# A bitonic sort of 2^18 keys on one core: mirrored merges, signs folded into the layout changes, and layout changes in quarters

## The chip, the cores and the metric

The kernel runs on one core of one Trainium2 chip. The metric is the time of one execution in microseconds (us), measured on the device. Every number below is a median over several executions, unless it is read from a profile; a profile shows one execution, and its span (first to last instruction) is about 2 us shorter than the measured time of the same execution.

Names: PE is TensorE for matmuls and PEld its weight loads, DVE is VectorE, ACT is ScalarE, POOL is GpSimd, SP is SyncE.

## The reference, cut to what matters

```python
N, E, D = 4096, 262144, 256
self_out = nodes @ w_self
msg = nodes[edges_src] @ w_msg
agg = np.zeros((N, D), np.float32)
np.add.at(agg, edges_dst, msg)          # a scatter-add over 262144 random edges
return self_out + agg
```

The kernel has no fast scatter-add. It packs every edge into one float key (destination and source bits), sorts the 262144 keys, and then walks over chunks of 128 sorted edges. For each chunk it builds two one-hot matrices on DVE and multiplies them on PE (the "one-hot stage"). The change concerns the sort, and what stands directly before and after it.

## The kernel before: the parts that matter

The keys lie in a tile of 128 partitions x 2048. In layout A a row (partition) holds 2048 neighbouring keys, so compare-exchange passes over index bits 0 to 10 are DVE work along a row. In layout B each 128x128 block is transposed, so bits 7 and higher lie along the row. Stage s of the bitonic sort merges over bits s-1 down to 0; from stage 11 on, the top bits need layout B and the low seven need layout A.

```python
def evac(out_ap, in_ap, g):                    # out of PSUM: ACT and DVE in turn
    if g % 2 == 0: nc.scalar.copy(out=out_ap, in_=in_ap)
    else:          nc.vector.tensor_copy(out=out_ap, in_=in_ap)

def switch_A_to_B():                           # switch_B_to_A is alike
    src = buf("A")
    dst3 = buf("B").rearrange("q (p g) -> q p g", g=G16)
    for g in range(G16):                       # 16 blocks of 128x128
        tp = psum.tile([P, P], FP32, name="tp_sw", tag="tp", bufs=4)
        nc.tensor.transpose(tp[:], src[:, g * P:(g + 1) * P], ident[:])
        evac(dst3[:, :, g], tp[:], g)

def flip(lay, blo, bhi):                       # negate half the keys, so that every
    ...                                        # comparison can run upwards
    nc.vector.tensor_scalar(out=reg, in0=reg, scalar1=-1.0, scalar2=None, op0=ALU.mult)

def cpass(lay, fb):                            # one pass: a min and a max, 128x1024 each
    ...
    nc.vector.tensor_tensor(out=lo_d, in0=lo_s, in1=hi_s, op=ALU.min)
    nc.vector.tensor_tensor(out=hi_d, in0=lo_s, in1=hi_s, op=ALU.max)

for s in range(1, NSTAGE + 1):                 # NSTAGE 18, JBITS 11
    if s <= JBITS - 1:
        flip("A", ...)
        for b in range(s - 1, -1, -1): cpass("A", b)
    else:
        switch_A_to_B(); flip("B", ...)
        for b in range(s - 1, 6, -1): cpass("B", b - 7)
        switch_B_to_A()
        for b in range(6, -1, -1): cpass("A", b)
switch_A_to_B()
```

After the sort, the first key of every 128-key chunk gives segment numbers. These go through DRAM to every partition; ACT counts signs; the counts become row indices; GpSimd gathers two sets of rows ("heads", `xh`); then the one-hot stage starts with the heads. A validity check of the kernel (`bad`, `bcol`, then a small DRAM round trip `fd` to `brow`, then `bsum`) stands in the same region.

Of the kernel before, what the change touches and what calls it, by code (L numbers as in the profile page):

```python
# [9 lines left out]
P = 128  # L10
FP32 = mybir.dt.float32
BF16 = mybir.dt.bfloat16
I32 = mybir.dt.int32
I64 = mybir.dt.int64

ALU = mybir.AluOpType
AX = mybir.AxisListType
ACTF = mybir.ActivationFunctionType
# [18 lines left out]
def _view3(ap: bass.AP, inner: int):  # L37
    return ap.rearrange("p (a b) -> p a b", b=inner)
# [3 lines left out]
def kernel(  # L42
# [9 lines left out]
    nc = tc.nc  # L52
# [4 lines left out]
    NCOL = E // P  # L57
# [3 lines left out]
    NSTAGE = 18  # L61
    JBITS = 11
    G16 = NCOL // P

    const = ctx.enter_context(tc.tile_pool(name="const", bufs=1))
    feat = ctx.enter_context(tc.tile_pool(name="feat", bufs=1))
    meta = ctx.enter_context(tc.tile_pool(name="meta", bufs=1))
# [10 lines left out]
    ident = const.tile([P, P], FP32, name="ident")  # L78
# [4 lines left out]
    Y = feat.tile([P, T, D], BF16, name="Y")  # L83


    sortp = tc.alloc_tile_pool(name="sortp", bufs=1)
    XA = [sortp.tile([P, NCOL], FP32, name=f"XA{i}") for i in range(2)]
    XB = [sortp.tile([P, NCOL], FP32, name=f"XB{i}") for i in range(2)]

    HC = NCOL // 2  # L90
    for h in range(2):
        d64 = XB[0][:].bitcast(I64)
        s64 = XB[1][:].bitcast(I64)
        nc.sync.dma_start(
            d64, edges_dst.rearrange("(p j) -> p j", p=P)[:, h * HC:(h + 1) * HC]
        )
        nc.scalar.dma_start(
            s64, edges_src.rearrange("(p j) -> p j", p=P)[:, h * HC:(h + 1) * HC]
        )
        dlo = d64.bitcast(I32)[:, 0::2]  # L100
        slo = s64.bitcast(I32)[:, 0::2]
        hi = XA[1][:].bitcast(I32)
        dhi = hi[:, 0:HC]
        shi = hi[:, HC:2 * HC]
        key = XA[0][:, h * HC:(h + 1) * HC]
        nc.vector.tensor_single_scalar(out=dhi, in_=dlo, scalar=9, op=ALU.logical_shift_right)
        nc.vector.tensor_single_scalar(out=shi, in_=slo, scalar=7, op=ALU.logical_shift_right)
        nc.vector.scalar_tensor_tensor(
            out=key, in0=dlo, scalar=128.0, in1=slo, op0=ALU.mult, op1=ALU.add
        )  # L110
        nc.vector.scalar_tensor_tensor(
            out=key, in0=dhi, scalar=float((1 << 21) - (1 << 16)), in1=key,
            op0=ALU.mult, op1=ALU.add,
        )
        nc.vector.scalar_tensor_tensor(
            out=key, in0=shi, scalar=float((1 << 16) - P), in1=key,
            op0=ALU.mult, op1=ALU.add,
        )


    ones_sent = const.tile([1, 1], FP32, name="ones_sent")
# [19 lines left out]
        out=hbase[:], in0=hbase[:], scalar1=float(SEGW), scalar2=None, op0=ALU.mult  # L141
# [6 lines left out]
        out=thr[:], in0=thr[:], scalar1=float(SEGW), scalar2=-0.5, op0=ALU.mult, op1=ALU.add  # L148
# [11 lines left out]
        pattern=[[0, NPER], [1, RING], [0, 8]], base=0, channel_multiplier=0,  # L160
# [19 lines left out]
    for t in range(T):  # L180
        y_ps = psum_y.tile([P, D], FP32, name="y_ps", tag="y_ps", bufs=2)
        for k in range(2):
            nc.tensor.matmul(  # L183
                out=y_ps[:], lhsT=XT[:, k, t * P:(t + 1) * P], rhs=wcat[:, 2 + k, :],
                start=(k == 0), stop=(k == 1),
            )
        nc.scalar.copy(out=Y[:, t, :], in_=y_ps[:])  # L187

    psum_sort = tc.alloc_tile_pool(name="psum_sort", bufs=1, space=bass.MemoryType.PSUM)
    srt, lane = _run_sort(nc, psum_sort, XA, XB, ident, NCOL, NSTAGE, JBITS, G16)  # L190


    k16 = meta.tile([P, G16], FP32, name="k16")
    k16i = meta.tile([P, G16], I32, name="k16i")
    kn = meta.tile([P, G16], FP32, name="kn")
    kni = meta.tile([P, G16], I32, name="kni")
# [13 lines left out]
    cnt = meta.tile([P, 2], FP32, name="cnt")  # L210
    cidx = meta.tile([P, 2], I32, name="cidx")

    tss = nc.vector.tensor_single_scalar
    tt = nc.vector.tensor_tensor
    nc.scalar.dma_start(xs_dram.rearrange("(p g) l -> p (g l)", g=G16), srt[:])
    nc.vector.tensor_copy(out=k16i[:], in_=srt[:, 0::P])
    tss(out=gi[:], in_=k16i[:], scalar=7, op=ALU.logical_shift_right)
    tss(out=dl[:], in_=gi[:], scalar=SEGW - 1, op=ALU.bitwise_and)
    nc.vector.tensor_scalar(
# [30 lines left out]
    rel_b = meta.tile([P, NCOL], BF16, name="rel_b")  # L250
    for q in range(NCOL // SBL):
        s = slice(q * SBL, (q + 1) * SBL)
        nc.vector.tensor_copy(out=ki[:, s], in_=lane[:, s])
        tss(out=kl[:, s], in_=ki[:, s], scalar=P - 1, op=ALU.bitwise_and)
        nc.scalar.copy(out=slo_b[:, s], in_=kl[:, s])
        tss(out=ki[:, s], in_=ki[:, s], scalar=7, op=ALU.logical_shift_right)
# [17 lines left out]
    for h in range(2):  # L274
        xh = meta.tile([P, P], FP32, name=f"xh{h}")
        nc.gpsimd.indirect_dma_start(
            out=xh[:], out_offset=None, in_=xs_dram[:, :],
            in_offset=bass.IndirectOffsetOnAxis(ap=cidx[:, h:h + 1], axis=0),
        )
        xt_ps = psum_sort.tile([P, P], FP32, name="xt_ps", tag="tp", bufs=4)  # L280
        nc.tensor.transpose(xt_ps[:], xh[:], ident[:])
        nc.vector.tensor_copy(out=hs_i[:, h * P:(h + 1) * P], in_=xt_ps[:])
    tss(out=hd_i[:], in_=hs_i[:], scalar=7, op=ALU.logical_shift_right)
    tss(out=hs_i[:], in_=hs_i[:], scalar=P - 1, op=ALU.bitwise_and)
    nc.vector.tensor_copy(out=hsl[:], in_=hs_i[:])
# [1 line left out]
    psum_sort.release()  # L287
    psum_y.release()
    stgn.release()
    sortp.release()  # L290

    for q in range(NCOL // SBL):
# [127 lines left out]
    brow = meta.tile([1, P], FP32, name="brow")  # L420
    bsum = meta.tile([1, 1], FP32, name="bsum")
    flag = meta.tile([1, 1], I32, name="flag")
    nc.vector.tensor_copy(out=k16[:], in_=k16i[:])
    nc.sync.dma_start(kd[0, 0:NCOL].rearrange("(p g) -> p g", g=G16), k16[:])
    nc.sync.dma_start(kn[:], kd[0, 1:NCOL + 1].rearrange("(p g) -> p g", g=G16))
    nc.vector.tensor_copy(out=kni[:], in_=kn[:])
# [88 lines left out]
            )  # L515


def _run_sort(nc, psum, XA, XB, ident, NCOL, NSTAGE, JBITS, G16):

    cur = {"A": 0, "B": 0}  # L520

    def buf(lay):
        return XA[cur[lay]][:, 0:NCOL] if lay == "A" else XB[cur[lay]][:, 0:NCOL]

    def other(lay):
        return XA[1 - cur[lay]][:, 0:NCOL] if lay == "A" else XB[1 - cur[lay]][:, 0:NCOL]

    def flip_live(lay):
        cur[lay] = 1 - cur[lay]

    def evac(out_ap, in_ap, g):
        if g % 2 == 0:
            nc.scalar.copy(out=out_ap, in_=in_ap)  # L533
        else:
            nc.vector.tensor_copy(out=out_ap, in_=in_ap)

    def switch_A_to_B():
        src = buf("A")
        dst3 = buf("B").rearrange("q (p g) -> q p g", g=G16)
        for g in range(G16):  # L540
            tp = psum.tile([P, P], FP32, name="tp_sw", tag="tp", bufs=4)
            nc.tensor.transpose(tp[:], src[:, g * P:(g + 1) * P], ident[:])  # L542
            evac(dst3[:, :, g], tp[:], g)

    def switch_B_to_A():
        src3 = buf("B").rearrange("q (p g) -> q p g", g=G16)
        dst = buf("A")
        for g in range(G16):
            tp = psum.tile([P, P], FP32, name="tp_sw2", tag="tp", bufs=4)
            nc.tensor.transpose(tp[:], src3[:, :, g], ident[:])  # L550
            evac(dst[:, g * P:(g + 1) * P], tp[:], g)

    def flip(lay, blo, bhi):
        x = buf(lay)
        if lay == "A":
            assert blo <= JBITS - 1 and (bhi is None or bhi <= JBITS - 1)
            base_lo = blo
        else:
            assert blo >= 7
            base_lo = blo - 7  # L560
            if bhi is not None:
                assert bhi == blo + 1
        if bhi is None:
            per = 1 << (base_lo + 1)
            reg = _view3(x, per)[:, :, (1 << base_lo):per]
        else:
            per = 1 << (base_lo + 2)
            reg = _view3(x, per)[:, :, (1 << base_lo):(3 << base_lo)]
        nc.vector.tensor_scalar(out=reg, in0=reg, scalar1=-1.0, scalar2=None, op0=ALU.mult)

    def cpass(lay, fb):
        src = buf(lay)
        dst = other(lay)
        per = 1 << (fb + 1)
        s3 = _view3(src, per)
        d3 = _view3(dst, per)
        lo_s = s3[:, :, 0:(1 << fb)]
        hi_s = s3[:, :, (1 << fb):per]
        lo_d = d3[:, :, 0:(1 << fb)]
        hi_d = d3[:, :, (1 << fb):per]  # L580
        nc.vector.tensor_tensor(out=lo_d, in0=lo_s, in1=hi_s, op=ALU.min)  # L581
        nc.vector.tensor_tensor(out=hi_d, in0=lo_s, in1=hi_s, op=ALU.max)  # L582
        flip_live(lay)

    for s in range(1, NSTAGE + 1):
        if s <= JBITS - 1:
            if s == 1:
                flip("A", 1, None)
            else:
                flip("A", s - 1, s)  # L590
            for b in range(s - 1, -1, -1):
                cpass("A", b)
        else:
            switch_A_to_B()
            if s == NSTAGE:
                flip("B", NSTAGE - 1, None)
            else:
                flip("B", s - 1, s)
            for b in range(s - 1, 6, -1):
                cpass("B", b - 7)  # L600
            switch_B_to_A()
            for b in range(6, -1, -1):
                cpass("A", b)

    switch_A_to_B()
    return XA[cur["A"]], XB[cur["B"]]


# [28 lines left out]
```

## Time and profile before

Time: 842.63 us (median of 3 runs, 841.58 to 842.98). The profiled execution has a span of 841.4 us.

These are two lines of the page's part 1 and part 2 for the kernel before. The first gives busy time, share of the span and instruction count per engine. The second is the TensorE clock that was granted, in tenths of full speed (9 is 90% or more), in 40 slices of 21 us each.

```profile
PE 337.7 (40%) x3730; PEld 268.0 (32%) x3730; DVE 772.9 (92%) x851; ACT 221.6 (26%) x449; POOL 15.1 (2%) x24
...
PEclk9999999999555555555555555589999999999999
```

DVE is busy 92% of the time, so DVE is the engine to relieve. The run of 5s says that PE works at about half clock from 210 us to the end of the sort. The clock is recorded only from its first rise on, here at 203 us, and what lies before that is shown as 9. The three switches before 203 us show the same spacing of their transposes, about 0.215 us, as those under the 5s, so they too ran at half clock.

A switch in detail: rows of the timeline of the kernel before (start in us, duration in us, engine, line, operation, output <- input). The last pass in layout B, two of the sixteen transposes, the last copy out of PSUM, and the first instruction of the next pass.

```profile
175.62 1.23 DVE L581 TENSOR_TENSOR XB_86<-XB_87 128x1024 f32<-128x1024 f32 x1
176.76 1.22 DVE L582 TENSOR_TENSOR XB_86<-XB_87 128x1024 f32<-128x1024 f32 x1
...
178.52 0.42 PE L550 MATMUL tp_sw_527<-ident,XB_86 128*128 128x128 f32 x1
...
178.74 0.42 PE L550 MATMUL tp_sw_530<-ident,XB_86 128*128 128x128 f32 x1
...
181.76 0.29 DVE L535 COPY XA_85<-tp_sw_563 128x128 f32<-128x128 f32 x1 [0.32 <-PE tp_sw_563 L550]
182.15 1.23 DVE L581 TENSOR_TENSOR XA_84<-XA_85 128x1024 f32<-128x1024 f32 x1
```

A pass repeats every 2.395 us (409.5 us for all 171). The pass at 175.62 would therefore be followed by another at 178.01; the next one comes at 182.15. So this B-to-A switch costs 4.14 us. An A-to-B switch costs 4.54, and a sign flip 0.73 beyond that. The transposes come every 0.21 to 0.22 us.

| part of the kernel before | us | how it is read |
|---|---|---|
| start, to the first flip | 24.0 | timeline |
| 171 passes | 409.5 | 171 x 2.395 |
| 18 flips | 13.1 | 18 x 0.73 |
| 16 layout switches | 69.4 | 8 x 4.14 + 8 x 4.54 |
| end of the last pass to the one-hots of the heads | 28.6 | 516.0 to 544.61 |
| one-hot stage | 296.8 | 544.61 to 841.4 |

Two more rows of the timeline of the kernel before, at the start: the shift L106 of the first key half waits 8.25 us for its load, and the first flip begins at 24.00.

```profile
8.25 1.31 DVE L106 TENSOR_SCALAR XA_85<-XB_86 128x1024 int32<-128x1024 int32 x1 [8.25 <-DMA XB_86<-in_edges_dst_dram]
...
24.00 0.70 DVE L569 TENSOR_SCALAR XA_84<-XA_84 128x1024 f32<-128x1024 f32 x1
```

And three at the end: the gather of the heads, the transpose that had to wait for its data, and the one-hot that ends the latency chain.

```profile
534.15 1.09 POOL L276 DMA_INDIRECT xh_1583<-xs_dram,cidx  x1 [520.10 <-DVE cidx L267]
...
541.62 0.45 PE L281 MATMUL xt_ps<-ident,xh_1583 128*128 128x128 f32 x1 [20.16 <-DMA xh_1583<-xs_dram,cidx]
...
544.61 1.20 DVE L310 TENSOR_TENSOR e_oh<-hsl,jrow 128x2048 bf16<-128x2048 bf16 x1
```

### The profile page before, as it was taken

The page shows a single profiled execution, that of the slowest core. Times are in us where ns is not written, and L with a number is a line of the kernel's source. Part 1 is how long each engine was busy: PE and PEld are TensorE (multiplying, and loading weights), DVE is VectorE, ACT ScalarE, POOL GpSimd, SP SyncE. Part 2 cuts the span into 40 slices and gives each one's busy share as a digit, 9 for nine tenths or more (in the row PEclk, how much of TensorE's full clock was granted, in tenths as well). Part 3 has the DMA queues.
Part 4 walks back from the last instruction along what each step waited for, and adds up shares of the span by engine and source line. Part 5 has one row for each costly group of instructions (what it writes and reads, how often), then busy time and mean ns, then how long its engine had stood idle before and what let it go on. Part 6 is the DMA issues. An engine that isn't in the chain of part 4 may idle for free. (4 is left out here: it accounts for less than half of the span.)

```text
span 841.4 us, 9662 instructions
## 1 busy us (share of the span) xinstructions
PE 337.7 (40%) x3730; PEld 268.0 (32%) x3730; DVE 772.9 (92%) x851; ACT 221.6 (26%) x449; POOL 15.1 (2%) x24
## 2 busy tenths in 40 slices
PE   0033320111111111111101112088888888888786
PEld 0000000111111111111101111076776777777675
DVE  3999999999999999999999998599999999999995
ACT  0011110111111111111101111245555555555454
POOL 6000000000000000000000000000000000000000
PEclk9999999999555555555555555589999999999999
DMA  8811100000000000000000002000000000000000
GB/s 238 177 27 25 27 19 0 0 1 1 0 0 0 0 0 0 1 0 0 0 0 0 0 0 102 7 2 26 3 27 2 26 2 27 26 2 26 2 26 28
DMA packets 25209, 17.89 MB, mean 21 GB/s; under 512 B 11557, under 2 KB 24358, under 8 KB 24390
## 3 DMA queue, kind: packets, MB, share of 16 engines
q1 hardware_dynamic: 19862, 11.59, 4.6%
q0 software_dynamic: 4720, 2.49, 2.2%
q10 hardware_dynamic: 578, 3.16, 0.9%
q8 instruction: 31, 0.51, 0.2%
q14 instruction: 18, 0.15, 0.1%
HBM read 10.12 MB, written 7.37 MB: 21 GB/s over the span
## 5 line engine op out<-in xcount | busy, mean ns | idle before, releaser
L342 ACT CAST at<-ring 128x512 bf16<-128x512 f32 x256 | 150.0, 587 | 144.9 <-PE ring L326 144.8
L326 PE MATMUL ring<-d_oh,e_oh 128*128 128x96 bf16 x2304 | 147.5, 208 | 44.6 <-DVE d_oh L310 38.4
L368 PE MATMUL out_ps<-Y,at 128*128 128x256 bf16 x1024 | 154.8, 274 | 0.0
L310 DVE TENSOR_TENSOR e_oh<-slo_b,jrow 128x2048 bf16<-128x2048 bf16 x128 | 154.3, 1206 | 0.0
L326 PEld LDWEIGHTS <-e_oh 128*128 128x128 bf16 x2304 | 132.2, 99 | 66.6 <-issue 48.1
L310 DVE TENSOR_TENSOR d_oh<-rel_b,jrow 128x1536 bf16<-128x1536 bf16 x128 | 120.3, 940 | 0.0
L368 PEld LDWEIGHTS <-at 128*128 128x128 bf16 x1024 | 86.5, 97 | 7.4 <-ACT at L342 0.6
L581 DVE TENSOR_TENSOR XA_85<-XA_84 128x1024 f32<-128x1024 f32 x56 | 68.6, 1225 | 2.2
L581 DVE TENSOR_TENSOR XA_84<-XA_85 128x1024 f32<-128x1024 f32 x55 | 67.4, 1225 | 2.2
L582 DVE TENSOR_TENSOR XA_85<-XA_84 128x1024 f32<-128x1024 f32 x56 | 68.3, 1219 | 0.0
L582 DVE TENSOR_TENSOR XA_84<-XA_85 128x1024 f32<-128x1024 f32 x55 | 67.0, 1219 | 0.0
L542 PE MATMUL tp_sw<-ident,XA_85 128*128 128x128 f32 x80 | 20.5, 436 | 111.3 <-DVE XA_85 L582 110.6
L183 PE MATMUL y_ps<-wcat,XT 128*128 128x256 bf16 x64 | 25.2, 394 | 96.3 <-DMA XT<-nodes_bf_dram 96.3
L542 PEld LDWEIGHTS tp_sw<-ident,XA_85 128*128 128x128 f32 x80 | 14.3, 193 | 117.4 <-DVE XA_85 L582 70.1
L533 ACT COPY XB_86<-tp_sw 128x128 f32<-128x128 f32 x40 | 15.1, 379 | 117.8 <-PE tp_sw L542 115.3
L542 PE MATMUL tp_sw<-ident,XA_84 128*128 128x128 f32 x64 | 16.0, 434 | 68.9 <-DVE XA_84 L582 68.9
L183 PEld LDWEIGHTS <-XT 128*128 128x128 bf16 x64 | 6.7, 104 | 114.6 <-DMA XT<-nodes_bf_dram 114.6
L581 DVE TENSOR_TENSOR XB_86<-XB_87 128x1024 f32<-128x1024 f32 x30 | 36.8, 1225 | 1.0
L581 DVE TENSOR_TENSOR XB_87<-XB_86 128x1024 f32<-128x1024 f32 x30 | 36.8, 1225 | 1.0
L187 ACT CAST Y<-y_ps 128x256 bf16<-128x256 f32 x32 | 11.9, 372 | 96.8 <-PE y_ps L183 96.8
L582 DVE TENSOR_TENSOR XB_87<-XB_86 128x1024 f32<-128x1024 f32 x30 | 36.6, 1219 | 0.0
L582 DVE TENSOR_TENSOR XB_86<-XB_87 128x1024 f32<-128x1024 f32 x30 | 36.6, 1219 | 0.0
(478 smaller groups left out, 287.3 us busy)
## 6 DMA issues: line engine op xcount, KB each, us to landing
out_dram<-o_sb SPq DMA_DIRECT2D x16, 256.0 KB, 2.3
XB_87<-in_edges_src_dram ACTq DMA_DIRECT2D x2, 1024.0 KB, 7.6
XB_86<-in_edges_dst_dram SPq DMA_DIRECT2D x2, 1024.0 KB, 7.5
nodes_bf<-in_nodes_dram POOLq DMA_DIRECT2D x1, 2048.0 KB, 18.1
nodes_bf_dram<-nodes_bf SPq DMA_DIRECT2D x1, 2048.0 KB, 8.7
XT<-nodes_bf_dram SPq DMA_TRANSPOSE x64, 2.4
xs_dram<-XA_85 ACTq DMA_DIRECT2D x1, 1024.0 KB
gball<-gd SPq DMA_DIRECT2D x1, 1024.0 KB, 4.7
```

The lines of the kernel that those rows point to most:

```text
L183: nc.tensor.matmul(out=y_ps[:], lhsT=XT[:, k, t * P:(t + 1) * P], rhs=wcat[:, 2 + k, :], start=(k == 0), stop=(k == 1),)
L187: nc.scalar.copy(out=Y[:, t, :], in_=y_ps[:])
L310: tt(out=o[:], in0=val.rearrange("p (g i) -> p g i", i=2).unsqueeze(2).to_broadcast(shp), in1=jrow[:, 0:wid, :].unsqueeze(1).to_broadcast( ...
L326: mm = nc.tensor.matmul(out=ap, lhsT=e[:, ci // 2, :, ci % 2], rhs=d[:, ci // 2, :, ci % 2], start=start, stop=True, skip_group_check=True ...
L342: ins = nc.scalar.copy(out=at[:], in_=ring[:, b:b + SEGW]).ins
L368: nc.tensor.matmul(out=out_ps[:, t, :], lhsT=at[:, t * P:(t + 1) * P], rhs=Y[:, b, :], start=False, stop=(b == T - 1), skip_group_check=True,)
L533: nc.scalar.copy(out=out_ap, in_=in_ap)
L542: nc.tensor.transpose(tp[:], src[:, g * P:(g + 1) * P], ident[:])
L581: nc.vector.tensor_tensor(out=lo_d, in0=lo_s, in1=hi_s, op=ALU.min)
L582: nc.vector.tensor_tensor(out=hi_d, in0=lo_s, in1=hi_s, op=ALU.max)
```

## The change

The intent has five parts:

- **No flips.** In layout A the first pass of a merge reads its second half backwards (a "mirrored" merge), so nothing has to be negated. For merges that begin in layout B the sign changes between stages are folded into the matrix that transposes: seven signed identities `sids`. The starting signs go into the key building (`ksg`).
- **Stage 11 inside a row.** The row merges now reach stage 11, which takes away one pair of switches.
- **No passes inside a chunk.** The order within 128 edges does not matter to the one-hot stage. The last merge stops after bit 7, and only the minimum of each chunk is taken after one last switch back. That takes away seven passes.
- **Switches in quarters.** The pass before a switch and the one after it are each split in four. Four plain f32 matmuls fill one PSUM bank (128x512), ACT copies it out in one instruction, and DVE starts on that quarter while PE works on the next.
- **Separate load buffers** for the two halves of the edges.

The core of the diff, cut, with some statements joined into fewer lines (`...` marks cuts):

```diff
+    for k in range(7):
+        nc.gpsimd.tensor_scalar(out=sids[k][:], in0=ident[:], scalar1=sgn[:, k:k + 1],
+                                scalar2=None, op0=ALU.mult)
...
+        nc.scalar.activation(out=key, in_=slo, func=ACTF.Copy, scale=ksg[:, 0:1])
+        tss(out=dhi, in_=dlo, scalar=9, op=ALU.logical_shift_right)
+        tss(out=shi, in_=slo, scalar=7, op=ALU.logical_shift_right)
+        for v, i in ((dlo, 1), (dhi, 2), (shi, 3)):
+            nc.vector.scalar_tensor_tensor(out=key, in0=v, scalar=ksg[:, i:i + 1], in1=key, ...)
...
+    for q in range(4):
+        _switch(nc, psum_sort, lane, srt, ident, q)
+        nc.vector.tensor_reduce(out=k16[:, 4 * q:4 * q + 4],
+            in_=_view3(srt[:, q * 512:(q + 1) * 512], P), axis=AX.X, op=ALU.min)
...
+def _switch(nc, psum, src, dst, rhs, q):
+    tp = psum.tile([P, 512], FP32, name="tp_sw", tag="tp", bufs=4)
+    for k in range(4):
+        c = slice((4 * q + k) * P, (4 * q + k + 1) * P)
+        nc.tensor.matmul(out=tp[:, k * P:(k + 1) * P], lhsT=src[:, c], rhs=rhs[:], start=True, stop=True)
+    nc.scalar.copy(out=dst[:, q * 512:(q + 1) * 512], in_=tp[:])
...
+    def cpass(src, dst, b, mirror=False, split=1):
+        ...
+            hi = s4[:, :, 1, ::-1] if mirror else s4[:, :, 1, :]
...
+    for s in range(1, JBITS + 1):                       # row merges, stages 1 to 11
+        for b in range(s - 1, -1, -1):
+            last = s == JBITS and b == 0
+            cpass(XA[a], XA[1 - a], b, mirror=(b == s - 1), split=4 if last else 1)
+    for s in range(JBITS + 1, NSTAGE + 1):              # stages 12 to 18
+        for q in range(4): _switch(nc, psum, XA[a], XB[b_], sids[s - JBITS - 1], q)
+        ...  cpass in B, first and last with split=4
+        if s == NSTAGE: return XB[b_]
+        for q in range(4): _switch(nc, psum, XB[b_], XA[a], ident, q)
+        for b in range(6, -1, -1): cpass(XA[a], XA[1 - a], b, split=4 if b in (0, 6) else 1)
```

After the change there are 164 passes and 13 switches in the sort, plus the last switch back for the minima.

## The prediction

It was written before the changed kernel had been run.

> **What bounds the kernel now.** By busy time per engine, VectorE (DVE) is busy 92% of 841 us. The timeline shows three stages. (1) To 24 us: load and key building, with DVE idle 8.3 and 4.9 us for loads. (2) 24 to 516: the sort, DVE in strict sequence. 171 passes of min+max (128x1024 f32, 1.22 us busy each, one pass every 2.395 us) = 409.5 us; 18 sign flips of 0.69 (pitch 0.73) = 13 us; 16 layout switches. From the last max to the next pass a B-to-A switch costs 4.1 us, an A-to-B switch 4.5 without its flip: 69 us. Sum 24+409.5+13+69 = 516. (3) 516 to 545: a latency chain (chunk keys, DRAM round trip, sign counts, indirect gather), then the one-hot stage to 841, DVE-bound (e_oh 1206 ns, d_oh 940 ns), which the change leaves alone.
>
> **Removed.** 18 flips: -13 us. The 7 passes inside a chunk of the last merge: -16.8. Three of the 16 mid-sort switches (stage 11 becomes a row merge; the last merge needs no way back): -13. Mirrored reads should cost what forward reads do: no pass shape in this trace differs from 1.22 us.
>
> **Switches, 13 left.** Each is now quarters: split last pass, four plain f32 matmuls, one ScalarE (ACT) copy 128x512 (0.59 us, as o_sb), split first pass. A 128x256 instruction should take about 0.345 us (estimate: the one-hot sizes give 1.04 ns per element at single rate, plus the 0.08 left of the 1.145 us pitch), so a split pass is 2.76 instead of 2.39. But the old transposes ran as transpose mode, one every 0.215 us at granted clock 0.50. The Trainium skill, "FP8 and Floating Point Precision", TensorE Precision Notes, gives true FP32 four passes: twice that, about 0.43 us (estimate), 6.8 us of TensorE (PE) per switch, so PE is the pace of the switch, not DVE. "TensorE: Matmul & The Clock Gate", Part 1, says sustained matmuls lift the clock after some 3.4 us and Part 4 that transposes don't count [...]; so the burst's end may run double. I estimate 3.5 us extra over two unsplit passes per switch (4.5 if always cold, 1.2 if always warm): 13 x 3.5 = 46 us against 69. The overlap itself gains only about 0.8 us per switch.
>
> **Start, a loss.** In the instruction order the sign constants sit behind the second key shift, and the seven signed identities on GpSimd (0.8 to 1 us each) come before the iota of 3.7 us that feeds a DRAM round trip, whose consumer (lom_c) stands before the first pass on DVE. First pass at about 30.5 instead of 24, although the loads no longer wait on each other.
>
> **End, a loss.** Chunk minima now need the final switch, and ACT runs three strided copies before its quarters 1 to 3: keys about 7 us after the last pass instead of at once; partly made up because counts no longer wait behind checks. Head one-hots about 34 us after the last pass (now 28.6).
>
> **Sum.** Last pass ends 30.5+164x2.395+0.4+46 = 469; +34+298 (rest, unchanged) = 801 us.
>
> Predicted 801 us, 80% range 780 to 822. Faster by over 2%: 0.93; within 2%: 0.06; slower: 0.01.
>
> **Shown right or wrong by:** sort passes still 1.22 us (mirrored too); f32 matmul pitch 0.43 us in the timeline of a switch; DVE idle 2.5 to 4 us per switch, released by ACT; idle before the first pass released by the lom_c DMA; one-hot stage still 296 us.
>
> **What would make it wrong:** weight loads of f32 not hidden (pitch 0.6: plus 35 us); clock warm through bursts (minus 28); negative steps slow (up to plus 25).

## The result, and the profile after

| kernel | median us (range, runs) | ratio to before (95% interval) |
|---|---|---|
| before | 842.55 (841.58 to 842.98, 4) | 1 |
| after | 798.91 (798.02 to 799.67, 4) | 0.9483 (0.9467 to 0.9500) |

A ratio here is the mean time of one kernel's fast runs over the mean time of the other's in the same rounds. It is therefore not quite the ratio of the two medians. All outputs are right. The changed kernel was run again in another series and gave 799.06 us, ratio 0.9475. The predicted 801 us was 2 us too high, well inside the range.

The same two lines of the page, for the kernel after:

```profile
PE 353.0 (44%) x3906; PEld 300.8 (38%) x3906; DVE 717.2 (90%) x859; ACT 215.9 (27%) x375; POOL 18.6 (2%) x32
...
PEclk9999999998666655556656655799999999999999
```

DVE has lost 56 us of work. The clock line now has 6s among the 5s: PE is granted more than half clock in parts of the sort. (Here too the record begins with the first rise, at 189.86 us.)

Groups by form of the kernel after, DVE, in the first 480 us: busy time and mean ns of one, then idle time before them and who ended it.

```profile
L578 DVE TENSOR_TENSOR XA<-XA 128x1024 f32<-128x1024 f32 x190 | 224.4, 1222 | 3.6
L578 DVE TENSOR_TENSOR XB<-XB 128x1024 f32<-128x1024 f32 x84 | 99.2, 1222 | 2.2 <-DVE XB L578 0.5
L578 DVE TENSOR_TENSOR XB<-XB 128x256 f32<-128x256 f32 x112 | 40.7, 421 | 17.7 <-ACT XB L559 16.6
L578 DVE TENSOR_TENSOR XA<-XA 128x256 f32<-128x256 f32 x104 | 37.7, 421 | 12.4 <-ACT XA L559 11.3
```

Twenty of the 190 instructions of the first line read one input backwards (the mirrored passes of stages 2 to 11; in stage 1 a block is one element long). The mean of their group, 1222 ns, is that of the second line, which has none of them, and no min or max of this kernel took more than 1227 ns, so mirrored reads cost nothing that shows. Most of the idle time stands before the quarter instructions, and ACT copies end most of that: 16.6 + 11.3 = 27.9 us.

The first switch, in the timeline of the kernel after:

```profile
185.17 6.05 PE L556 MATMUL tp_sw<-sid,XA 128*128 128x128 f32 x32 [52.02 <-DVE XA L578]
187.26 0.58 ACT L559 COPY XB<-tp_sw 128x512 f32<-128x512 f32 x1 [53.70 <-PE tp_sw L556]
187.87 0.76 DVE L578 TENSOR_TENSOR XB<-XB 128x256 f32<-128x256 f32 x2 [0.84 <-ACT XB L559]
188.96 0.58 ACT L559 COPY XB<-tp_sw 128x512 f32<-128x512 f32 x1 [1.12 <-PE tp_sw L556]
...
190.36 0.58 ACT L559 COPY XB<-tp_sw 128x512 f32<-128x512 f32 x1 [0.81 <-PE tp_sw L556]
...
191.26 0.58 ACT L559 COPY XB<-tp_sw 128x512 f32<-128x512 f32 x1 [0.31 <-PE tp_sw L556]
```

The record says x32 for 16 blocks: a plain f32 matmul leaves two records per block, a transpose before left one. DVE waits for ACT, and ACT waits for PE, so PE sets the pace. The copies come 1.70, 1.40 and 0.90 us apart. A quarter of four blocks takes 1.70 us at half clock, 0.43 us per block, and half of that once the clock has risen, 4.7 us into this burst. The Trainium skill, "FP8 and Floating Point Precision", TensorE Precision Notes, says that true FP32 takes four passes; the traces agree: at full clock a block takes 0.223 us here, and the bf16 matmuls of experiment 3, 512 columns each, follow one another every 0.216 us at full clock, which is 0.054 us for 128 columns (an estimate). In transpose mode before, a block took half as long as here at the same half clock (0.215 against 0.43 us). The Trainium skill, "TensorE: Matmul & The Clock Gate", Part 1, gives about 3.4 us of sustained matmuls before the full clock; in the kernel after the rise comes 3.1 to 6.1 us after a burst's start, over its 14 bursts, which is in line with that page's remark that the window runs freely.

The start, in the timeline of the kernel after:

```profile
14.75 4.45 POOL L115 TENSOR_SCALAR sid<-ident,sgn 128x128 f32<-128x128 f32 x7 [10.12 <-DVE sgn L102]
...
19.76 3.72 DVE L176 TENSOR_SCALAR lo_c<-c_i 128x16 int32<-128x16 int32 x1 [4.28 <-POOL c_i L175]
19.79 3.66 POOL L182 IOTA r_i<- 1x2112 int32 x1
20.18 3.32 DVE L179 TENSOR_SCALAR hi_c<-c_j 128x16 int32<-128x16 int32 x1
...
23.57 4.93 DVE L140 SCALAR_TENSOR_TENSOR XA<-XB,ksg,XA 128x1024 f32<-128x1024 int32 x4
...
28.42 0.16 DVE L190 TENSOR_TENSOR lom_c<-lo_c,lo 128x16 int32<-128x16 int32 x1
```

DVE waits 4.28 us for a tiny iota that stands behind the seven identities on GpSimd, and then two tiny instructions last as long as the big iota beside them. The `lom_c` instruction, the consumer of the DRAM round trip, shows no wait. The first pass begins at 28.53. The end, in the same timeline:

```profile
464.24 6.44 PE L556 MATMUL tp_sw<-ident,XB 128*128 128x128 f32 x32 [23.70 <-DVE XB L578]
...
492.42 0.28 DVE L484 TENSOR_REDUCE bsum<-brow 1x1 f32<-1x128 f32 x1 [7.42 <-DMA brow<-fd]
...
493.43 1.06 POOL L308 DMA_INDIRECT xh<-xs_dram,cidx  x1 [466.08 <-DVE cidx L299]
...
496.27 0.45 PE L313 MATMUL xt_ps<-ident,xh 128*128 128x128 f32 x1 [25.59 <-DMA xh<-xs_dram,cidx]
...
499.43 1.23 DVE L343 TENSOR_TENSOR e_oh<-hsl,jrow 128x2048 bf16<-128x2048 bf16 x1
```

The last pass ends at 466.44, the head one-hots begin at 499.43. Between 28.53 and 466.44 lie 437.9 us; 164 x 2.395 = 392.8 of them are passes, and the remaining 45.1 belong to the 13 switches, 3.47 each. That gives the balance:

| part | before, us | after, us | difference |
|---|---|---|---|
| start, to the first flip or pass | 24.0 | 28.5 | +4.5 |
| passes | 409.5 | 392.8 | -16.7 |
| flips | 13.1 | 0 | -13.1 |
| layout switches | 69.4 (16) | 45.1 (13) | -24.3 |
| last pass to head one-hots | 28.6 | 33.0 | +4.4 |
| one-hot stage | 296.8 | 296.8 | 0 |
| span | 841.4 | 796.2 | -45.2 |

So the gain lies where the arithmetic put it, and 9 us of it is given back at the two ends. What the balance cannot tell is why a switch costs 3.47 us, and why the two ends are longer. The experiments ask that.

### The profile page after: what moved, and what is told of

Read it like the earlier page. It is cut to its first block, busy times and chain, and to the rows that moved or that the text cites. A ratio compares the mean times of both kernels' runs of the same rounds, so it can differ in the third digit from the quotient of the medians.

```text
span 796.2 us, 10040 instructions
## 1 busy us (share of the span) xinstructions
PE 353.0 (44%) x3906; PEld 300.8 (38%) x3906; DVE 717.2 (90%) x859; ACT 215.9 (27%) x375; POOL 18.6 (2%) x32
## 5 line engine op out<-in xcount | busy, mean ns | idle before, releaser
L578 DVE TENSOR_TENSOR XA<-XA 128x1024 f32<-128x1024 f32 (+1 forms) x294 | 262.1, 939 | 16.1 <-ACT XA L559 11.3
L578 DVE TENSOR_TENSOR XB<-XB 128x256 f32<-128x256 f32 (+1 forms) x196 | 139.9, 764 | 19.9 <-ACT XB L559 16.6
L556 PE MATMUL tp_sw<-sid,XA 128*128 128x128 f32 x224 | 41.7, 372 | 138.6 <-DVE XA L578 138.6
L556 PEld LDWEIGHTS tp_sw<-sid,XA 128*128 128x128 f32 x224 | 40.6, 285 | 139.8 <-issue 139.8
L556 PE MATMUL tp_sw<-ident,XB 128*128 128x128 f32 x224 | 41.6, 371 | 115.7 <-DVE XB L578 115.7
L556 PEld LDWEIGHTS tp_sw<-ident,XB 128*128 128x128 f32 x224 | 40.4, 284 | 116.8 <-issue 116.8
L559 ACT COPY XB<-tp_sw 128x512 f32<-128x512 f32 x28 | 16.4, 585 | 164.2 <-PE tp_sw L556 164.2
L559 ACT COPY XA<-tp_sw 128x512 f32<-128x512 f32 x28 | 16.3, 586 | 138.2 <-PE tp_sw L556 138.2
L343 DVE TENSOR_TENSOR e_oh<-hsl,jrow 128x2048 bf16<-128x2048 bf16 x16 | 19.5, 1219 | 0.0
L343 DVE TENSOR_TENSOR d_oh<-hrel,jrow 128x1536 bf16<-128x1536 bf16 x16 | 15.2, 951 | 0.0
## 6 DMA issues: line engine op xcount, KB each, us to landing
nodes_bf<-in_nodes_dram POOLq DMA_DIRECT2D x1, 2048.0 KB, 16.1
```

Source lines behind the costliest of these rows:

```text
L343: tt(out=o[:], in0=val.rearrange("p (g i) -> p g i", i=2).unsqueeze(2).to_broadcast(shp), in1=jrow[:, 0:wid, :].unsqueeze(1).to_broadcast( ...
L556: nc.tensor.matmul(out=tp[:, k * P:(k + 1) * P], lhsT=src[:, c], rhs=rhs[:], start=True, stop=True)
L559: nc.scalar.copy(out=dst[:, q * 512:(q + 1) * 512], in_=tp[:])
L578: nc.vector.tensor_tensor(out=d4[:, :, t, :], in0=s4[:, :, 0, :], in1=hi, op=op)
```

## The experiments

The theory after reading the two traces: inside a switch PE is the pace, because a plain f32 matmul takes twice the time of a transpose and most of a burst runs at half clock. The rivals: the ACT copies or the split DVE instructions are the pace; or the quarters do not overlap as intended. For the start, the theory is that DVE waited behind the identities on GpSimd; the rival is the prediction's own, that the round trip of `lom_c` through DRAM released the first pass. For the end, the theory is an order of instructions in which the counts wait behind the check; the rival is the prediction's, ACT's strided copies.

### 1. The changed kernel without the overlap

```diff
-            cpass(XA[a], XA[1 - a], b, mirror=(b == s - 1), split=4 if last else 1)
+            cpass(XA[a], XA[1 - a], b, mirror=(b == s - 1), split=1)
```

and likewise for the other two places with `split=4`.

> The changed kernel without the overlap: every pass whole (split=1), the switches still four f32 matmuls and one ACT copy per quarter. Theory (PE is the pace of a switch, so the quarters hide about half of its 5.3 to 6.4 us burst): first pass after a switch starts about 6.6 us after the last one ends, against 3.4 us of extra time per switch now; 13 switches x 3.2 us = 42 us slower than the changed kernel, plus 2 in the final switch: about 843 us, no faster than the kernel before. Rival (the matmuls are fast enough and DVE and ACT set the pace, the splitting itself is worth about 1 us per switch): about 812 us.

Measured: 839.13 us (837.53 to 840.46, 4 runs), ratio 0.9951 (0.9935 to 0.9968). The waits of DVE in this kernel between 24 and 545 us (total us, times, longest):

```profile
DVE XB L578 <- ACT XB L559: 49.7, 7, 7.3
DVE XA L578 <- ACT XA L559: 35.3, 6, 6.4
```

The total is 4 us less than the 843 that the theory named, and nearly all of the change's gain is gone. Without the split DVE stands still for the whole burst at each of 13 switches, 85 us in all and up to 7.3 at a time. With it, 27.9 us were left, at most 0.9 at a time. The quarters are worth 40 us to the kernel after: without them, the switch from transposes to plain matmuls would have eaten nearly all that the removed flips and passes gave. Net of the extra cost of a split pass (2.77 us against 2.395, as the last pass in the trace of after shows), the overlap works as designed.

### 2. Transpose mode for the switches that carry no signs

```diff
         nc.tensor.matmul(out=tp[:, k * P:(k + 1) * P], lhsT=src[:, c], rhs=rhs[:], start=True, stop=True,
+            is_transpose=plain,
```

with `plain=True` for the six B-to-A switches and the last one.

> The seven switches from layout B to A, which multiply by the plain identity, put back into transpose mode; the seven signed ones stay plain f32 matmuls. Theory (PE passes are the pace): PE spacing per 128-block falls from 0.43 to 0.215 us, each of the 6 B-to-A switches in the sort gains 2.0 to 2.3 us and the final one about 3: 15 us less, about 784 us; signed switches unchanged. Rival (ACT copies or DVE quarters are the pace): under 3 us.

Measured: 780.13 us (779.34 to 781.66, 4 runs), ratio 0.9261. One B-to-A burst in its timeline:

```profile
199.83 3.71 PE L556 MATMUL tp_sw<-ident,XB 128*128 128x128 f32 x16 [9.21 <-DVE XB L579]
```

And DVE's waits for ACT's copies in the sort of this kernel (total us, times, longest):

```profile
DVE XB L579 <- ACT XB L560: 15.2, 20, 0.9
```

Sixteen records instead of 32, 3.71 us instead of some 6. DVE's waiting for the copies into XA is gone altogether, and 15.2 us for XB, still plain matmuls, remain. With the same ACT copies and the same DVE instructions, PE's shorter burst alone took the wait away. That excludes ACT and DVE as the pace. The gain of 18.8 us is more than the 15 expected. In the two profiles 14.2 us of it lie in the sort and 3.4 between the last pass and the heads. The last switch, whose burst took 6.44 us in the kernel after, has its part in the 3.4, but not alone: in this build DVE runs the counts before the check (`cidx` at 469.30, `bsum` at 479.64), though the edit does not touch that order. The builds of experiments 3 and 7 have this order too. So for the switches the gain in the sort, first pass to last against the profile of after, is the clean figure: 14.2 us here, 24.3 in experiment 3 and 29.1 in experiment 7.

### 3. The clock kept up between the switches

After each switch, matmuls that feed nothing run into a spare PSUM tile while DVE does its passes:

```diff
+    def keep_warm(mm, passes):
+        n = int((2.3 + 2.395 * (passes - 2) - 1.0) / 0.216)
+        for _ in range(n):
+            nc.tensor.matmul(out=wps[:], lhsT=wcat[:, 0, 0:P], rhs=wcat[:, 0:2, :], ...)
```

> The changed kernel, with bf16 matmuls on constants into a spare PSUM bank after each switch, counted so that they end about 1 us before the next switch; they feed nothing. Theory (most of each burst runs at granted clock 0.5): bursts shrink from 5.3-6.4 to about 3.5 us, extra time per switch from 3.4 to about 1.2 us for 12 switches, the final one gains about 3: 28 to 30 us less, about 770 us. Rival (the burst is bound by loading f32 weights or by ACT, not by the clock): under 5 us, or slower because the extra matmuls delay the real ones.

Measured: 771.00 us (769.90 to 771.60, 4 runs), ratio 0.9145. Windows view from 192 to 440 us (length, then busy time and count of PE, PEld, DVE, ACT, POOL, then granted clock, DMA share, GB/s) of this kernel, then of the kernel after:

```profile
192.00:440.00 248.00, 234.26 (x1259) 128.37 (x1257) 239.86 (x340) 28.69 (x49) 0.00 (x0) 1.00 0.00 1
```

```profile
192.00:440.00 248.00, 70.27 (x381) 68.53 (x382) 217.72 (x316) 27.20 (x47) 0.00 (x0) 0.63 0.00 0
```

And a burst of this kernel, in its timeline:

```profile
201.67 3.86 PE L556 MATMUL tp_sw<-ident,XB 128*128 128x128 f32 x32 [0.79 <-DVE XB L579]
```

And all that is left of DVE's waits for copies in the sort (total us, times, longest):

```profile
DVE XB L579 <- ACT XB L559: 3.1, 4, 0.9
```

The clock is 1.00 instead of 0.63, a burst of the same 32 records takes 3.86 us, and DVE's waits for ACT shrink from 27.9 to 3.1 us, all of them at the first, still unwarmed switch. So the two factors of PE's time, records per block and clock, are shown one by one: halving either one makes PE fast enough that DVE no longer waits.

### 4. The start put in another order

The signs are built while DVE still waits for the loads, the identities come after the iotas, and the halves are finished one after the other:

```diff
+    # order edge: the shifts of a key half come after the signs, or after the half before
+        for x in (i0, i1):
+            tc.add_manual_dep(x, kins.ins.name, nosync, reason="signs, then the half before")
-    for k in range(7): nc.gpsimd.tensor_scalar(out=sids[k][:], ...)      # here, before the iotas
+    for k in range(7): nc.gpsimd.tensor_scalar(out=sids[k][:], ...)      # after them
```

> Only the start reordered: the seven signed identities on GpSimd after the iotas, sign constants before the key shifts on DVE, keys half by half. Theory A (the start lost time because the constants, then the c_i and r_i iotas, came late, and DVE stood still under the iota): first pass starts at about 20 us instead of 28.5, total about 790 us; the two small DVE ops that took 3.7 and 3.3 us fall under 0.5. Theory B (as predicted: only the round trip to DRAM for lom_c counts): first pass at about 21 to 22 too, but the two small ops unchanged where an iota runs beside them. Rival C (the loads of 4 MB bound the start): first pass at 26 or later, total over 796.

Measured: 792.98 us (792.34 to 793.62, 4 runs), ratio 0.9407. In its timeline:

```profile
10.15 0.36 DVE L177 TENSOR_SCALAR lo_c<-c_i 128x16 int32<-128x16 int32 x1
...
12.54 11.21 POOL L205 TENSOR_SCALAR sid<-ident,sgn 128x128 f32<-128x128 f32 x7
...
20.97 6.07 DVE L584 TENSOR_TENSOR XA<-XA 128x1024 f32<-128x1024 f32 x5
```

The first pass starts at 20.97 instead of 28.53. The `lom_c` round trip is still there. It causes a wait of only 0.38 us here and none in the kernel after, so it was not the cause. Of the 7.56 us won at the start 5.9 arrive in the total. DVE's waits at the switches were 30.9 us in this profile against 27.9 in after; a repeat of after showed 29.8. The PE bursts differ in the same way: summed over the 13 switches they take 76.9 us in after, 78.4 in its repeat and 79.4 here, because the clock rises at other points of the bursts. The repeat without any edit varies as well, so this part of the difference need not come from the edit.

### 5. The check moved behind the heads

```diff
-    nc.vector.tensor_reduce(out=bsum[:], in_=brow[:], axis=AX.X, op=ALU.add)
+    bs = nc.vector.tensor_reduce(out=bsum[:], in_=brow[:], axis=AX.X, op=ALU.add)
+    tc.add_manual_dep(bs.ins, hsl_ins.ins.name, ..., reason="heads before the check")
```

> The changed kernel with one order forced on DVE: the sum of the check (bsum, which waits for a round trip of 512 bytes to DRAM) after the head keys instead of before the counts. Theory (DVE stood 7.4 us at bsum, with the counts and the indirect gather behind it): counts at about 486 us instead of 493; the gather may take up to 7 us, as in the kernel before, because the same small write is then still under way, so the heads come 4 to 7 us earlier: total 792 to 795 us. Rival (the gather would only wait for the same DMA queues, so the stall costs nothing): within 1.5 us of 799.

Measured: 793.19 us (792.06 to 794.79, 5 runs), ratio 0.9417 (0.9404 to 0.9430); that is 5.7 us less than after. (The two profiled executions, the fastest of after and the slowest of this kernel, differ by only 3.2 us, as do their head one-hots.) In its trace `bsum` comes at 495.96, after the last key of the heads, the gather is issued at 488.50 (in after 493.43), and the head one-hots start at 496.16. So the wait of 7.42 us at `bsum` in after did stand in the chain. Not all of it comes back. Counted from the last pass, the gather is issued 7.4 us earlier, but the second gather takes longer than in after: the transposes come at 491.25 and 494.08, 2.8 and 4.2 us after the issue of their gathers, where after had 2.8 and 2.6.

### 6. The passes inside a chunk put back

Seven passes over bits 6 to 0 after the final switch, the first and last split in four:

```diff
+    for i, b in enumerate(range(6, -1, -1)):
+        ...   # min and max from XA[i % 2] to XA[1 - i % 2]
```

> The changed kernel with the seven passes inside a chunk put back, in the row layout after the final switch, before the chunk minima. Theory (they lie wholly on the critical path): 7 x 2.395 = 16.8 us, plus 0.7 for two split passes, minus up to 1.5 because the first split pass hides behind the final switch: total 814 to 816 us. Rival (the final burst of PE and the three ACT copies hide part of them): under 810 us.

Measured: 812.88 us (811.61 to 813.54, 4 runs), ratio 0.9649. That is 14.0 us more than after, not the 16.8 of seven passes, and a little under the expected range: a miss. The first of the seven is split, and its quarters run at 467.9 to 473.6 us, mostly under the final PE burst and the copies, which DVE would have waited for anyway. The wait at `bsum` is also shorter, 5.86 us instead of 7.42. Leaving out work next to a wait gains less than its own length.

### 7. Transposes everywhere, signs in the copies

If PE is the pace at two records per block, the signs should not travel through the matmul. Here the signed identities are gone, all switches are transposes, and the sign is given by the copy out of PSUM, which then needs two ACT instructions per quarter:

```diff
+    for c in range(4):
+        nc.tensor.transpose(tp[:, c * P:(c + 1) * P], src[:, (4 * q + c) * P:(4 * q + c + 1) * P], ident[:])
+    nc.scalar.copy(out=o4[:, :, plus, :], in_=i4[:, :, plus, :])
+    nc.scalar.activation(out=o4[:, :, minus, :], in_=i4[:, :, minus, :], func=ACTF.Copy, scale=-1.0)
```

> All 13 switches and the final one in transpose mode with the plain identity; the signs of the seven A-to-B switches go into the ACT copies out of PSUM (two instructions of 256 elements per quarter, one with scale -1) instead of signed identities. Theory (plain f32 matmuls at the half clock were the pace): every switch falls to what the B-to-A switches showed in the run with transposes, about 0.8 us extra, so 7 x 2.3 to 2.6 us less than that run's 780, and the identities vanish from GpSimd before the first pass (2 to 4 us): 758 to 764 us. Rival (two ACT copies per quarter, on interleaved elements, take over as the pace at over 0.9 us per quarter): 768 us or more.

Measured: 759.48 us (759.38 to 759.87, 4 runs), ratio 0.9020 (0.9007 to 0.9034). An A-to-B switch in its timeline:

```profile
180.38 3.65 PE L548 MATMUL tp_sw<-ident,XA 128*128 128x128 f32 x16 [62.98 <-DVE XA L579]
181.50 0.40 ACT L559 COPY XB<-tp_sw 128x256 f32<-128x256 f32 x1 [63.70 <-PE tp_sw L548]
181.79 0.41 ACT L560 ACTIVATE XB<-tp_sw 128x256 f32<-128x256 f32 x1
182.23 13.30 DVE L579 TENSOR_TENSOR XB<-XB 128x256 f32<-128x256 f32 x22
```

DVE starts the new pass at 182.23 and works on for 13.3 us. The list of DVE's waits has no wait for a copy in this kernel's sort. The clock still stays at half in most slices (5s in the clock line). The Trainium skill, "TensorE: Matmul & The Clock Gate", Part 4, says that the full clock does not engage for transposes; this trace does not bear that out. PE runs nothing but transposes in this sort, and yet the granted clock rises to 1.00 eight times, 2.9 to 4.1 us after the start of a burst and for 3.4 us each time; in three bursts the last transposes still profit, at 0.11 us from one to the next. The trace of before has five such rises in its sort. Bursts of 3.4 to 3.7 us end before the rise or just after it, so it brings them little. (The clause of the prediction that had the trace of before at 0.50 throughout is cut above for this reason.) It does not matter any more. PE and ACT deliver a quarter every 0.85 us, DVE uses one up in 2.77 / 4 = 0.69, and the split of the pass before gives PE a start of 1.85 us (180.38 to 182.23). The sort takes 408.9 us (23.75 to 432.60), 16.1 more than its 164 passes: 1.2 per switch, of which 0.75 is the price of two split passes (2 x (2.77 - 2.395)).

This kernel also separates the causes at the start, because its start differs from after's only in having no identities. Its first key product starts at 16.46 (after: 20.26) and its first pass at 23.75 (after: 28.53). So of 4.78 us, 3.80 are DVE's wait behind the identities, and 0.98 are lost between the first product and the first pass, where in after the iota ran beside them.

### 8. All of it together

Experiment 7 with the start order of 4 and the order of the check of 5.

> Transposes with signs folded into the ACT copies, start reordered, check after the heads, all together. If the three causes are separate, their gains add: the folded version less about 4 (start, part of which the vanished identities already gave) less 4 to 7 (end): 749 to 756 us. If they hide one another: over 758.

Measured: 754.63 us (754.45 to 754.76, 4 runs), ratio 0.8961 (0.8947 to 0.8975). It lies in the expected range, near its upper end. Of the 4.9 us below experiment 7, 3.0 are won at the start (first pass at 20.76 instead of 23.75). That leaves 1.9 for the new order at the end, which gave 5.7 in experiment 5. One reason is that in experiment 7 the counts already stood before the check: its gather was issued at 450.56, before `bsum` at 459.57, so there was less to win. The timeline of experiment 8 shows the other:

```profile
446.10 0.32 SPq L483 DMA_DIRECT2D fd<-bcol  x1
...
447.54 1.08 POOL L309 DMA_INDIRECT xh<-xs_dram,cidx  x1 [434.13 <-DVE cidx L300]
...
452.87 0.24 SPq L484 DMA_DIRECT2D brow<-fd  x1
...
453.15 0.45 PE L314 MATMUL xt_ps<-ident,xh 128*128 128x128 f32 x1 [22.16 <-DMA xh<-xs_dram,cidx]
```

The gather is issued 1.4 us after the check's small write (`fd`, 128 x 4 bytes) and takes 5.6 us. The transpose of its rows starts 0.28 us after the read `brow` was issued, which waits for that write to land. In the kernel before the pattern is the same: `fd` at 533.62, the gather at 534.15, `brow` issued at 541.37, the heads at 541.62. (Experiments 2, 3 and 7 show it too, each with 0.25 us.) That made a new theory: a gather that starts while the small write is under way is as slow as the write.

### 9. The small write behind the gather

Experiment 8, with `bcol` (and so `fd`) after the heads, and `bsum` in the midst of the one-hot stage:

```diff
+    tc.add_manual_dep(bc.ins, hsl_ins.ins.name, ..., reason="heads before the check")
+    tc.add_manual_dep(bs.ins, oh_ins[60].name, ..., reason="check in the one-hot stage")
```

> The version with all three repairs, with the check's column sum, its 512-byte write (fd) and the sum that waits for its way back (bsum) moved behind the head keys and into the one-hot stage. Theory (in two runs the indirect gather of the heads landed only when that small write had landed, 0.3 us after it, however early it was issued): the gather lands 2.7 to 3.5 us after its issue, as in the changed kernel where the write had landed before, so the heads come about 3 to 4 us earlier: 750 to 752 us. Rival (the gather itself takes 4 to 7 us whenever it is issued right after the sign counts): 754 to 755 us, unchanged.

Measured: 751.89 us (751.54 to 752.23, 5 runs), ratio 0.8916 (0.8904 to 0.8928).

```profile
447.87 1.08 POOL L309 DMA_INDIRECT xh<-xs_dram,cidx  x1 [434.49 <-DVE cidx L300]
...
450.63 0.45 PE L314 MATMUL xt_ps<-ident,xh 128*128 128x128 f32 x1 [19.36 <-DMA xh<-xs_dram,cidx]
```

With the write moved away, the gather takes 2.8 us, and the total falls by 2.7 us. That the write delays the gather is shown; by which queue or memory it does so is not. This is the best version found; it beats the kernel before by 91 us and the kernel after by 47.

### 10. The changed kernel once more

For an anchor in the series of experiment 9, the changed kernel was run again.

> The changed kernel unaltered once more, as an anchor in the same series as the last version: 798 to 800 us; anything else would mean that the series can't be compared across chips to a few us.

Measured: 799.06 us (798.73 to 800.03, 4 runs), ratio 0.9475 (0.9461 to 0.9490), the same as the first time.

## Why the prediction was right, point by point

| step | predicted | measured |
|---|---|---|
| first pass | 30.5 us | 28.53 |
| 164 passes of 2.395 us, mirrored ones too | 392.8 | 1222 ns per instruction, unchanged |
| 13 switches | 0.4 + 46 | 45.1 |
| last pass ends | 469 | 466.44 |
| head one-hots after the last pass | about 34 | 33.0 |
| one-hot stage | unchanged, 296 | 296.8 in both |
| total | 801 | 798.91 |

The total was right for a good reason in its largest parts. The flips, the seven passes and the three switches left with the time that the trace of before gave to them. The step that carried the risk was "so PE is the pace of the switch, not DVE", with 0.43 us per block and a clock that may rise during the burst. The trace shows 0.43 us and the rise, and experiments 2 and 3 show each of the two factors alone. The predicted 3.5 us per switch was 3.47.

Three steps failed, although their sizes came out close:

- **The start.** The prediction said "idle before the first pass released by the lom_c DMA". No instruction waited for that DMA in the kernel after. Its size was a loss of 6.5 us, and 4.5 were measured. The seven identities on GpSimd, which waited themselves for signs that DVE built late, held back a tiny iota `c_i`, and DVE waited 4.28 us for that one in program order. After that, the large iota `r_i` ran beside DVE: two conversions that take 0.17 us in the kernel before have records of 3.72 and 3.32 us, and end about when the iota ends. The Trainium skill, "SBUF — State Buffer", SBUF: two separate sides, says that DVE in some modes and GpSimd take a shared port pair as an exclusive lock for a whole instruction. The two long records fit such a block, yet the time lost was only about 1.0 us (experiment 7): the next key products have records that start at 20.26, inside the iota, and the third starts right after it, at 23.57. So DVE's work did not stand still for 3.7 us; how much of it the lock held up is not shown. A long record is not the same as a loss of that length. The identities also took 0.64 us each rather than the assumed 0.8 to 1, as long as DVE was idle; beside a busy DVE (experiment 4) they took 1.6 each.
- **The end.** The prediction put the loss on ACT's "three strided copies before its quarters 1 to 3" and counted on a gain "because counts no longer wait behind checks". In the trace the final PE burst takes 6.44 us, at half clock nearly to its end (32 records of 0.213 us would be 6.8), and delivers its last quarter at about 470.7; the last copy, at 471.24, is only half a microsecond behind. So ACT was not the cause of more than that. And the counts did wait behind the check, 7.42 us, as experiment 5 shows by taking it away. The size came out because another term, the gather, was shorter than in the kernel before (2.8 against 7.5 us from issue to transpose): it now ran after the check's small write had landed. Two errors of similar size (5.7 us by experiment 5, and 4.6 us between the two gathers) had opposite signs; that the sum came out was luck.
- **The overlap.** "The overlap itself gains only about 0.8 us per switch" is right as a net figure against the old switch (4.14 to 4.54 against 3.47), and hides what happens. The old switches were transposes, and the plain f32 matmuls that took their place cost more: the quarters win (839.1 - 798.9) / 13 = 3.1 us per switch over the changed kernel without them, so some 2.3 us of that (3.1 - 0.8, an estimate) only pay for the matmuls. The change was paid for by the overlap, and experiment 7 shows that the payment was avoidable: signs in the copies cost nothing that DVE could feel, and that kernel is 39 us faster (29.1 of it in the sort, 4.8 at the start, and 4.1 between the last pass and the heads, where the order of the check had changed as well).

## What to carry to other kernels

When a step is folded into another engine's work, count that engine's work at the clock it will really have: here folding signs into a matmul turned one PE record per block into two at half clock, while folding them into the ACT copy was free. Split both passes around a layout change, since that alone was worth 40 us here, and then ask which engine ends the remaining wait; halving PE's time, by mode or by clock, took nearly all of it away. And look at the instruction order at the two ends of a stage: a wait for a side result (a check, an iota) in the order of a busy engine can delay all that follows like a real dependency (5.7 us here by the check), and a tiny scattered DRAM write in front of a gather can cost as much as the gather (2.7 us here).

## What the Trainium skill lacked or had wrong

- "TensorE: Matmul & The Clock Gate", Terms, calls transpose mode four times faster for FP32. Measured at the same half clock, a 128x128 f32 block takes 0.215 us in transpose mode and 0.43 us as a plain f32 matmul: a factor of two. The measurement decides for this kernel. The sentence of Part 4 on the clock of transposes does not hold here either: see experiment 7, with eight rises to 1.00 in a sort that has only transposes.
- "Vector Engine (DVE) Microarchitecture Reference", section 5.1, lists streaming with a negative step as not measured. Here a 128x1024 f32 min or max whose second input is read backwards takes 1222 ns (the mean of its group, with no instruction above 1227), as forwards.
- "SBUF — State Buffer" names the exclusive lock between DVE and GpSimd; it does not say what it looks like in a trace. Here DVE instructions of 0.17 us have records of 3.72 us, for as long as an iota on one partition lasts (3.66 us), while only about 1.0 us was lost. In the other direction, a 128x128 f32 tensor_scalar on GpSimd took 0.64 us beside an idle DVE and 1.6 us beside a busy one.
- "DMA: Bandwidth & Descriptors" has no figure for a write of 128 pieces of 4 bytes to DRAM, nor for what it does to a gather that comes after it: here 6.8 to 8.0 us from its issue to the issue of the read that waits for it, and 5.6 to 7.7 us, up to the transpose of the rows, for a gather that is issued 0.5 to 1.4 us after the write, against 2.8 us with the write moved away (experiment 9) or landed before (the kernel after). A gather issued 4.5 us after the write (experiment 5) took 2.8 us, and the next one 4.2.
